# Fixed distances modulo 256 bytes between tokens, high weights and low weights in a one-core decoder layer

## The chip, the core and the metric

One core of a Trainium2 chip runs the whole layer as one program. The metric is the device time of that program in microseconds, the median over runs. A second number used below is the span of one profiled execution, from its first instruction to its last.

## The reference, cut to what matters

One decoder layer on 256 prompt tokens and 8 sample tokens, all in float32, with a model width of 2048 (16 chunks of 128).

```python
def layer(x, ...):
    xn = rmsnorm(x, g_mix)
    z = xn @ w_in                                   # all inputs of both groups
    ... RG-LRU group -> y_rg, mLSTM group -> y_ml ...
    x = x + jnp.concatenate([y_rg, y_ml], axis=-1) @ w_out
    xq = (rmsnorm(x, g_xa) @ w_xa_q)                # cross attention, 4 heads, 256 memory rows
    ...
    x = x + o @ w_xa_o
    xf = rmsnorm(x, g_ffn)
    x = x + (jax.nn.silu(xf @ w_ffn_gate) * (xf @ w_ffn_up)) @ w_ffn_down
    return x
# memory keys and values: mn @ w_k, mn @ w_v;  y = rmsnorm(x, g_final)
```

Nearly all the arithmetic is in products of a token matrix (264 columns: 256 prompt and 8 sample tokens) with a weight matrix of 128 output columns per step.

## The kernel before

**Three products for one.** Each float32 operand is split into a high part in the tensor engine's reduced float32 type and a low part that is the remainder. A product is the sum of three matmuls (`mm3`, L179): high weights with high tokens, high weights with low tokens, low weights with high tokens. In each matmul the 128x128 block of weights is loaded into the array and 264 token columns are streamed through it. Below, one *chunk* is the group of three matmuls of one 128-row block of the contraction; a step has 16 chunks (12 in the last part of the feed-forward).

**Steps.** The list `steps` holds one entry for each 128 output columns of a weight matrix (1 MB, `raw`). `load_piece` fetches it on SyncE's queue into one of three buffers, three steps ahead. `split_half(i, h)` converts it one step ahead, in two halves of 1024 columns: ScalarE writes the high half `wh`, then VectorE writes the low half `wl = raw - wh`. Each half is a tile of its own, four buffers for `wh` and four for `wl`, so a half is free again as soon as the tensor engine has used its eight chunks. `proj` (L819) walks the chunks in their natural order 0 to 15. The results are taken out of PSUM (`evac`, residual adds, gates) one step later. Between the steps `pump` hands out slices of side work (RG-LRU, mLSTM, decode attention) to ScalarE and VectorE; the framework's scheduler then fixes one order of instructions per engine.

**Where the operands lie.** A token array (`Arr`, `HL`) is cut into tiles of four chunks, `[128, 4, 264]` float32. One chunk is 1056 bytes, which is 4 x 256 + 32: the place of a chunk in its tile (its number modulo four) shifts it by 32 bytes modulo 256. All these tiles come from one ring of 26 buffers of 4224 bytes (tag `B`), which is 16.5 x 256, so that neighbouring buffers differ by 128 bytes modulo 256. A weight chunk is 512 bytes, and `wh` and `wl` tiles are 4096 bytes: in the built program every weight chunk, high or low, starts at 224 modulo 256. So the *distance*, the start of the streamed tokens less the start of the weights, modulo 256, runs through all multiples of 32, by the place of the chunk and by the buffers that the high and the low token tiles happened to get. In the text a chunk is named by the two distances of its high and its low tokens, such as (192, 64).

**Memory rows.** The 256 memory tokens use the same buffers with a chunk of 1024 bytes, so that there the distance is the same for all four chunks of a tile. In the value projections (`pe_v`) the roles are exchanged: memory rows are the loaded operand and 512 weight columns are streamed.

Two more names: `evac_rgg` and `rg_out` sum squares in `acc_rg`, the residual adds in `acc_x`; `tmp` gives short-lived tiles from a ring of `NT` buffers.

Of the kernel before, what the change touches and what calls it, by code (L numbers as in the profile page):

```python
# [10 lines left out]
F32 = mybir.dt.float32  # L11
F32R = mybir.dt.float32r
I32 = mybir.dt.int32
AF = mybir.ActivationFunctionType
# [3 lines left out]
P = 128  # L18
D = 2048
KC = D // P  # L20
T = 256
NS = 8
N = T + NS
# [57 lines left out]
def layer_kernel(ctx: ExitStack, tc, xT, memT, vec, wrg, w_in, w_out, w_q, w_k, w_v, w_o,  # L81
# [3 lines left out]
    act, dve, pe = Engine(nc.scalar, price_act), Engine(nc.vector, price_dve), Engine(nc.tensor, price_pe)  # L85
    pool_e, sp = nc.gpsimd, nc.sync
# [20 lines left out]
    def ltmp(w=N):  # L107
        return tmp(w, "lt")

    class Arr:  # L110


# [2 lines left out]

        def tile(self, q):
            if q not in self.t:
                self.t[q] = B([P, min(4, self.nb), self.w], self.dt)
            return self.t[q]

        def __call__(self, c):
            return self.tile(c // 4)[:, c % 4, :]

    class HL:
        def __init__(self, nb, w=N):
# [11 lines left out]
    steps = []  # L137
    LD, LS = 3, 1

    raws, splits = {}, {}  # L140

    def load_piece(i):
        if i >= len(steps) or i in raws:
# [6 lines left out]
    def split_half(i, h, parts=1):  # L150
        if i >= len(steps):
            return
        if steps[i][2] is pe_if:
            if h == 0:
                split_gates(i)
            return
        cols = steps[i][1]
        lo, hi = h * 1024, min(cols, (h + 1) * 1024)
# [3 lines left out]
        n = (hi - lo) // parts  # L162
        with tc.high_priority():
            for o in range(0, hi - lo, n):
                st["split"] = act.activation(wh[:, o: o + n], r[:, lo + o: lo + o + n], AF.Copy)
                dve.tensor_sub(wl[:, o: o + n], r[:, lo + o: lo + o + n], wh[:, o: o + n])
        splits[i, h] = (wh, wl)

    class W:
        def __init__(self, i):  # L170
            self.i = i

        def __call__(self, c, w=P):
            per = 1024 // w
            wh, wl = splits[self.i, c // per]
# [59 lines left out]
    def bank(tag="mm"):  # L235
        return psm.tile([P, 512], F32, tag=tag, bufs=4, name=nm(tag))

    warm_act = const.tile([P, 1], F32, name="warm_act")
    act.activation(warm_act, ones[:, 0:1], AF.Square)

    def warm(n, w=None):

# [262 lines left out]

    def split_gates(i):

        r = raws[i]
        for h in range(2):
            w = sb.tile([P, 8, P], F32R, tag="wh", bufs=4, name=nm("wh"))  # L510
            x = r[:, h * 1024: h * 1024 + 1024].rearrange("p (c m) -> p c m", m=P)
            with tc.high_priority():
                act.activation(w[:, :, 0:64], x[:, :, 0:64], AF.Copy)
                dve.tensor_sub(w[:, :, 64:128], x[:, :, 0:64], w[:, :, 0:64].bitcast(F32))
            splits[i, h] = w

    def pe_if(i):
        ps = bank()
        for c in range(KC):
            w = splits[i, c // 8][:, c % 8, :]  # L520
            xh, xl = rx(c)
            pe.matmul(ps[:, :N], w, xh, start=c == 0, stop=False)
            pe.matmul(ps[:, :N], w, xl, start=False, stop=c == KC - 1)
        return ps

    def evac_if(ps):
# [79 lines left out]
    def evac_v(j):  # L606
        def f(ps):
            if j == 0:
                ml["v"] = Arr(8)
            dve.tensor_mul(ml["v"](j), ps[:, :N], rstd)  # L610
            ml["vn"] = j + 1
        return f
# [203 lines left out]
            split(*st["yml"](j), z, V("g_ml", j))  # L816
        return f

    def proj(src, rhs, evac, cols=2048, n=N, need=()):  # L819
# [26 lines left out]
    for q in range(4):  # L846
        steps.append((w_in[q], 2048, pe_first(q), evac_first if q == 3 else None, ()))
    for n in range(4, RGB):
        proj(w_in[n], rx, evac_rgx(n))
    steps.append((w_in[8], 2048, pe_if, evac_if, ()))  # L850
    for j in range(8):
        proj(w_in[9 + j], rx, evac_qk(j))
    for j in range(8):
        proj(w_in[17 + j], rx, evac_v(j))
    for n in range(RGB):
        proj(w_in[25 + n], rx, evac_rgg(n), need=("rg",))
    for j in range(8):
        proj(w_in[33 + j], rx, evac_o(j))

# [21 lines left out]
    def final(m):  # L881

        def f(ps):
            x = xres[:, m, :]
            if m == 0:
                st["y"] = Arr(KC)
            dve.tensor_add(x, x, ps[:, :N])
            if m < KC - 1:
                sumsq(acc_x, x, m == 0)
            else:  # L890
                warm(4)
                sq = tmp()
                with tc.high_priority():
                    act.activation(sq, x, AF.Square)
                fin_sums(fin["sum"], sq, False)
            act.activation(st["y"](m), x, AF.Copy, scale=V("g_final", m))
            if m == 0:
                act.activation(warm_act, acc_x[:, 0:1], AF.Sqrt)
            elif m == KC - 2:
                fin["sum"] = bank("ax")  # L900
                fin_sums(fin["sum"], acc_x, True)
            elif m == KC - 1:
                rstd_fin(fin["sum"])
        return f

    def mem_gen():
        raw = Arr(KC, T)
        for i in range(4):
            pool_e.dma_start(raw.tile(i), memT[:, i * 4: i * 4 + 4, :])
        yield STEP  # L910
        yield STEP
        acc = ltmp(T)
        for c in range(KC):
            sumsq(acc, raw(c), c == 0)
            yield 0.35
        r = ltmp(T)
        yield STEP
        yield from rstd_from(acc, r, D)
        st["mem"] = HL(KC, T)
        for c in range(KC):  # L920
            x = raw(c)
            dve.tensor_mul(x, x, r)
            split(*st["mem"](c), x, V("g_mem", c))
            yield 0.7
# [3 lines left out]

    for m in range(KC):
        proj(w_out[m], ry, residual(m, "g_xa", "xa", norm_x),  # L930
             need=("rgout",) if m == 0 else ())

# [77 lines left out]

    rq = lambda c: st["xa"](c)
    for j in range(KC):
        proj(w_q[j], rq, evac_q(j), need=("rstd_xa",) if j == 1 else ())

    rm = lambda c: st["mem"](c)
    kv = {}
# [46 lines left out]

    def attend(h):
        qh, ql = B([P, 4, T], F32R), B([P, 4, T], F32R)
        q = qn["t"].tile(h)
        act.activation(qh, q, AF.Copy)
        dve.tensor_sub(ql, q, qh.bitcast(F32))  # L1070
        yield 1.2
# [49 lines left out]

    for h in range(H):
        for j in range(4):
            proj(w_k[4 * h + j], rm, evac_k(h, j), n=T, need=("memg",))
        for k4 in range(4):
            steps.append((w_v[h, k4], 2048, pe_v(h, k4), evac_vm(h) if k4 == 3 else None, ()))

    def ro(c):
        return st["o"](c)
# [6 lines left out]
    def pe_o(m):  # L1136
        def f(i):
            ps = bank()
            w = W(i)
            if m >= 2:  # L1140
                for c in range(KC):
                    mm3(ps[:, :N], w(c), ro(c), c == 0, c == KC - 1)
                return ps
            held[m] = (ps, w)
            for c in range(12):
                mm3(ps[:, :N], w(c), ro(c), c == 0, False)
# [49 lines left out]
    for part, nf in enumerate(FPARTS):  # L1196
        for j in range(nf):
            proj(w_gu[2 * (f0 + j)], rf, evac_gate(f0 + j, part, j),
                 need=("rstd_ffn",) if part == 0 and j == 1 else ())
            proj(w_gu[2 * (f0 + j) + 1], rf, evac_up(part, j))  # L1200
        wd = (w_d0, w_d1, w_d2)[part]
        ra = lambda c, part=part: st["a", part](c)
        lastp = part == 2
        for m in range(KC):
            proj(wd[m], ra, final(m) if lastp else residual(m, None, None, None), cols=nf * P)
        f0 += nf


# [171 lines left out]
```

## Time and profile before

| what | value |
|---|---|
| runs shown (three) | 1572.96, 1575.18, 1575.92 us; median 1575.18 |
| the profiled execution's own time | 1576.51 us |
| its span | 1574.8 us |
| granted TensorE clock, mean | 0.991 |
| matmuls busy / weight loads busy | 99% / 97% of the span |
| VectorE / ScalarE / GpSimd busy | 67% / 50% / 7% |
| 264-column matmuls with projection weights | 10,496 in groups of `wh` and `wl` |

In the rows of a group the order is: line, engine, operation, output<-inputs, shapes, count, then busy microseconds, the mean of one in ns, idle time before it and what ended that. Nearly every operation stands under line 60, since the class `Engine` records them there, so groups are told apart by tile names. The mean of one matmul (285 ns) is its latency; matmuls overlap, and what counts is the distance of their starts. Rows of the timeline give the start, the duration, and a count where equal neighbours are merged: `wh ... x2` is the first two matmuls of a chunk, so its start is the start of the chunk.

### The profile page before, as it was taken

Reading aid. Unit: us, or ns where it says so; the run is one execution under the profiler, and the core shown is the slowest. Engines: PE = TensorE matmul, PEld = TensorE weight load, DVE = VectorE, ACT = ScalarE, POOL = GpSimd, SP = SyncE. Lnnn points to the kernel's source line nnn. Section 1 sums busy time; section 2 is a strip of 40 time slices with the busy share of each in tenths; the row PEclk is TensorE's granted clock in tenths of the full one; section 3 lists DMA queues with packets and bytes.
Section 4 is the critical chain, followed back from the end, with each engine's and each line's share of the span. In section 5 each row is a group of like instructions: output and inputs, shape, how many; then the busy total and the mean of one; then the engine's idle time right before and its main releaser. Section 6 shows DMA issues by size and latency. Waiting matters only on the chain.

```text
span 1574.8 us, 29829 instructions
## 1 busy us (share of the span) xinstructions
PE 1556.5 (99%) x12340; PEld 1532.6 (97%) x12340; DVE 1051.4 (67%) x2021; ACT 789.7 (50%) x1252; POOL 109.6 (7%) x174
## 2 busy tenths in 40 slices
PE   9999999999999999999999999999999999999997
PEld 8999999999999889999999999999999999999997
DVE  7876877787699899956655555455555554555554
ACT  7465675565455656645444444333444433344463
POOL 0001210000124333200000000000000000000000
PEclk9999999999999999999999999999999999999998
DMA  8455875546689788745545555555455554555452
GB/s 304 161 174 172 294 269 205 178 145 245 248 321 346 302 305 319 251 161 178 187 164 185 188 180 175 181 188 186 174 179 186 187 181 172 184 188 184 156 179 99
DMA packets 55303, 325.97 MB, mean 207 GB/s; under 512 B 6688, under 2 KB 7120, under 8 KB 24448
## 3 DMA queue, kind: packets, MB, share of 16 engines
q1 hardware_dynamic: 39744, 270.68, 48.4%
q0 software_dynamic: 15136, 53.16, 9.4%
q8 instruction: 96, 1.57, 0.4%
q14 instruction: 39, 0.32, 0.1%
q10 hardware_dynamic: 288, 0.23, 0.1%
HBM read 312.78 MB, written 11.28 MB: 206 GB/s over the span
## 4 chain that ended last, share of the span: by engine, by line
PE 94%; DMA 2%; DVE 2%; ACT 1%; issue 1%; DVEq 0%; POOL 0%; SPq 0%; ACTq 0%
PE mm L60 89%; PE ax L60 4%; DVE B L60 1%; DMA o_sc<-B 1%; ACT B L60 1%; DMA raw<-w_in 1%; ACT wh L60 0%; DMA B<-scr 0%; DVE wl L60 0%; ACT L60 0%; DMA vecs<-vec 0%; DMA scr<-lt 0%; DVE t L60 0%; DVE dw L60 0%; ACT t L60 0%
## 5 line engine op out<-in xcount | busy, mean ns | idle before, releaser
L60 PE MATMUL mm<-B,wh 128*128 128x264 f32 (+1 forms) x7520 | 1379.0, 285 | 4.8 <-DVE B L60 3.0
L60 PEld LDWEIGHTS mm<-B,wh 128*128 128x128 f32 x7520 | 1168.4, 189 | 6.4 <-ACT cso L60 3.1
L60 PE MATMUL mm<-B,wl 128*128 128x264 f32 (+1 forms) x3744 | 1062.8, 284 | 0.6 <-DVE wl L60 0.6
L60 ACT ACTIVATE wh<-raw 128x1024 fp32r<-128x1024 f32 (+2 forms) x518 | 536.9, 1038 | 692.0 <-PE mm L60 574.6
L60 DVE TENSOR_TENSOR wl<-raw,wh 128x1024 fp32r<-128x1024 f32 (+2 forms) x516 | 619.0, 1201 | 356.7 <-ACT wh L60 350.0
L60 PEld LDWEIGHTS mm<-B,wl 128*128 128x128 f32 x3744 | 706.7, 189 | 1.1 <-DVE wl L60 1.0
L60 DVE TENSOR_TENSOR t<-mm,rstd 128x264 f32<-128x264 f32 x104 | 44.9, 432 | 60.2 <-PE mm L60 60.2
L60 PE MATMUL mm<-wh,B 128*128 128x512 f32 x256 | 82.3, 395 | 0.0
L60 DVE TENSOR_TENSOR xres<-xres,mm 128x264 f32<-128x264 f32 x80 | 34.2, 428 | 47.1 <-PE mm L60 47.1
L1272 POOL TENSOR_TENSOR B<-B,rstd 128x264 f32<-128x264 f32 x4 | 2.8, 743 | 864.9 <-ACT rstd L60 864.9
L60 PEld LDWEIGHTS mm<-wh,B 128*128 128x128 f32 x256 | 47.8, 189 | 9.8
L60 DVE SCALAR_TENSOR_TENSOR B<-B,dw 128x256 f32<-128x256 f32 x128 | 52.6, 465 | 2.3 <-ACT dw L60 2.3
L60 PE MATMUL mm<-wl,B 128*128 128x512 f32 x128 | 50.6, 395 | 0.0
L60 DVE SCALAR_TENSOR_TENSOR dw<-B,qsm,dw 128x256 f32<-128x256 f32 x96 | 47.9, 500 | 1.4 <-ACT dw L60 0.7
L60 PE MATMUL ax<-B,B 128*128 128x256 f32 (+3 forms) x288 | 48.2, 308 | 0.3 <-DVE B L60 0.3
L60 PEld LDWEIGHTS ax<-B,B 128*128 128x128 f32 x288 | 40.8, 189 | 4.0 <-issue 1.2
L977 POOL TENSOR_TENSOR ds<-dw,ds 128x256 fp32r<-128x256 f32 x32 | 35.4, 1107 | 115.3 <-ACT ds L60 115.2
L60 ACT ACTIVATE B<-xres,vecs 128x264 fp32r<-128x264 f32 (+1 forms) x64 | 31.1, 503 | 2.5 <-DMA xres<-xT 1.4
L60 ACT ACTIVATE t<-xres 128x264 f32<-128x264 f32 x60 | 23.9, 413 | 15.4 <-DVE xres L60 15.4
L60 PEld LDWEIGHTS mm<-wl,B 128*128 128x128 f32 x128 | 24.1, 188 | 5.0
L966 POOL DMA_DIRECT2D B<-kcT x32 | 17.5, 546 | 147.4 <-DVE B L60 127.0
L60 DVE TENSOR_TENSOR acc_x<-acc_x,t 128x264 f32<-128x264 f32 x59 | 25.2, 428 | 0.9 <-ACT t L60 0.5
(157 smaller groups left out, 740.0 us busy)
## 6 DMA issues: line engine op xcount, KB each, us to landing
raw<-w_gu SPq DMA_DIRECT2D x88, 1024.0 KB, 4.8
raw<-w_in SPq DMA_DIRECT2D x40, 1024.0 KB, 4.9
raw<-w_d SPq DMA_DIRECT2D x32, 1024.0 KB, 4.8
raw<-w_out SPq DMA_DIRECT2D x16, 1024.0 KB, 4.8
B<-kcT POOLq DMA_DIRECT2D x32, 512.0 KB, 6.1
raw<-w_q SPq DMA_DIRECT2D x16, 1024.0 KB, 5.0
B<-vcT POOLq DMA_DIRECT2D x32, 512.0 KB, 7.2
raw<-w_k SPq DMA_DIRECT2D x16, 1024.0 KB, 6.4
```

What stands on the lines that cost most here:

```text
L60: return f(*a, **k)
L966: pool_e.dma_start(kc, kcT[h, b])
L977: pool_e.tensor_sub(ws[:, 1], acc, ws[:, 0].bitcast(F32))
L1272: e.tensor_mul(st["y"](c), st["y"](c), r)
```

## The change

Token tiles are put into buffers of 4352 bytes (17 x 256), 64 bytes from the start. A step's whole weights are one `wh` and one `wl` tile of 8448 bytes (33 x 256), two buffers each, with the low weights 128 bytes from the start; in a tile the chunks stand in four groups by their number modulo four, each group 2080 bytes (8 x 256 + 32) after the last. The order of the chunks in a step goes group by group, forward in one step and backward in the next. In the built program all `B`, `wh` and `wl` buffers start at 160 modulo 256, so each chunk has a distance of 64 between tokens and high weights and of 192 (that is, minus 64) between tokens and low weights, whatever its place. Value projections keep natural columns (`wide`). To make room `NT` goes from 6 to 5 and `acc_rg` becomes another name of `acc_x`.

```diff
+    BW, XO = 1088, 16
+    WW, LO = 2112, 32
...
-                self.t[q] = B([P, min(4, self.nb), self.w], self.dt)
+                t = B([P, BW], self.dt)
+                self.t[q] = t[:, XO: XO + 4 * N].rearrange("p (c n) -> p c n", n=N)
...
-    NB, NT, NL, NFL = 26, 6, 3, 2
+    NB, NT, NL, NFL = 26, 5, 3, 2
...
-        wh = sb.tile([P, 1024], F32R, tag="wh", bufs=4, name=nm("wh"))
-        wl = sb.tile([P, 1024], F32R, tag="wl", bufs=4, name=nm("wl"))
+        if h == 0:
+            splits[i] = wtiles()
+        wh, wl = splits[i]
...
+        h4, l4 = wgroups(wh), wgroups(wl)
+        x = r.rearrange("p (q j m) -> p q j m", j=4, m=P)
+        q0, q1 = h * 2, min(cols // (4 * P), h * 2 + 2)
+        n = (q1 - q0) // parts or 1
         with tc.high_priority():
-            for o in range(0, hi - lo, n):
-                st["split"] = act.activation(wh[:, o: o + n], r[:, lo + o: lo + o + n], AF.Copy)
-                dve.tensor_sub(wl[:, o: o + n], r[:, lo + o: lo + o + n], wh[:, o: o + n])
-        splits[i, h] = (wh, wl)
+            for q in range(q0, q1, n):
+                k = slice(q, min(q + n, q1))
+                st["split"] = act.activation(h4[:, k], x[:, k], AF.Copy)
+                dve.tensor_sub(l4[:, k], x[:, k], h4[:, k].bitcast(F32))
+
+    def wtiles():
+        wh = sb.tile([P, WW], F32R, tag="wh", bufs=2, name=nm("wh"))
+        wl = sb.tile([P, WW], F32R, tag="wl", bufs=2, name=nm("wl"))
+        return wh[:, 0: 4 * GW], wl[:, LO: LO + 4 * GW]
+
+    GW = 4 * P + 8
+
+    def wgroups(t):
+        return t.rearrange("p (j g) -> p j g", g=GW)[:, :, 0: 4 * P].rearrange("p j (q m) -> p q j m", m=P)
+
+    def order(n, back=False):
+        return [c for j in (range(3, -1, -1) if back else range(4)) for c in range(j, n, 4)]
...
-            o = (c % per) * w
+            o = c * w if w != P else c % 4 * GW + c // 4 * P
...
-    acc_rg = const.tile([P, N], F32, name="acc_rg")
+    acc_rg = acc_x
...
-            for c in range(nch):
-                mm3(ps[:, :n], w(c), rhs(c), c == 0, c == nch - 1)
+            for k, c in enumerate(order(nch, back)):
+                mm3(ps[:, :n], w(c), rhs(c), k == 0, k == nch - 1)
```

The tensor engine, a gate or up step of the feed-forward, its first four chunks. `B` tiles hold four chunks of tokens each (1208, 1231 and so on are the high parts of the four quarters before, 995, 1012, 1034 and 1056 after; the next number is the low part). Before:

```order
L60 MATMUL mm_1347_9862<-B_1208_8715,wh_1337_9795 128x264
L60 MATMUL mm_1347_9862<-B_1209_8716,wh_1337_9795 128x264
L60 MATMUL mm_1347_9862<-B_1208_8715,wl_1338_9796 128x264
L60 MATMUL mm_1347_9862<-B_1208_8715,wh_1337_9795 128x264
L60 MATMUL mm_1347_9862<-B_1209_8716,wh_1337_9795 128x264
L60 MATMUL mm_1347_9862<-B_1208_8715,wl_1338_9796 128x264
```

After:

```order
L60 MATMUL mm_1098_9607<-B_995_8496,wh_1092_9544 128x264
L60 MATMUL mm_1098_9607<-B_996_8497,wh_1092_9544 128x264
L60 MATMUL mm_1098_9607<-B_995_8496,wl_1093_9545 128x264
L60 MATMUL mm_1098_9607<-B_1012_8691,wh_1092_9544 128x264
L60 MATMUL mm_1098_9607<-B_1013_8692,wh_1092_9544 128x264
L60 MATMUL mm_1098_9607<-B_1012_8691,wl_1093_9545 128x264
L60 MATMUL mm_1098_9607<-B_1034_8945,wh_1092_9544 128x264
L60 MATMUL mm_1098_9607<-B_1035_8946,wh_1092_9544 128x264
L60 MATMUL mm_1098_9607<-B_1034_8945,wl_1093_9545 128x264
L60 MATMUL mm_1098_9607<-B_1056_9199,wh_1092_9544 128x264
```

The number and kind of the matmuls are the same. Before, the second chunk of a step is the neighbour in the same token tile; now it is the chunk of the same place in the next tile, and the third chunk already needs the second half of the weights.

ScalarE in the output projection of the cross attention, two steps each, with what an instruction waits for. `wh ...` are the two halves of a step's conversion, `B` and `t` the tokens for the next norm's products and their squares; `PE_49`, `DVE_49` and `Activation_49` are the engines' own counters, `DMAHW...` a landed load. Before:

```order
L60 ACTIVATE wh_1285_9380<-raw_1276_9307 128x1024 [waits DMAHW2_49,PE_49,Activation_49]
L60 ACTIVATE wh_1287_9384<-raw_1276_9307 128x1024 [waits PE_49,Activation_49]
L60 ACTIVATE B_1261_9178<-xres_91,vecs_88 128x264 [waits DVE_49]
L60 ACTIVATE t_1284_9377<-xres_91 128x264
L60 ACTIVATE wh_1294_9447<-raw_1283_9372 128x1024 [waits DMAHW3_49,PE_49,Activation_49]
L60 ACTIVATE wh_1296_9451<-raw_1283_9372 128x1024 [waits PE_49,Activation_49]
```

After:

```order
L60 ACTIVATE wh_1015_8698<-raw_1006_8625 128x2x4x128 [waits DMAHW3_49,PE_49]
L60 ACTIVATE B_1012_8691<-xres_91,vecs_88 128x264 [waits DVE_49]
L60 ACTIVATE t_1014_8695<-xres_91 128x264 [waits DMASW7_49]
L60 ACTIVATE wh_1015_8698<-raw_1006_8625 128x2x4x128 [waits DVE_49]
L60 ACTIVATE wh_1020_8761<-raw_1011_8688 128x2x4x128 [waits DMAHW4_49,PE_49]
L60 ACTIVATE B_1012_8691<-xres_91,vecs_88 128x264 [waits DVE_49]
L60 ACTIVATE t_1019_8758<-xres_91 128x264 [waits DMASW0_49]
L60 ACTIVATE wh_1020_8761<-raw_1011_8688 128x2x4x128 [waits DVE_49]
```

Before, each half waits for the tensor engine by itself. Now the first half waits for the tensor engine's last use of the whole tile, and the second half, in the same tile, waits for VectorE: its counter value is the subtraction of the first half (`wl` reads the first half of `wh`).

More of the change, by code (lines that the diff above doesn't have):

```diff
@@ L138, in layer_kernel @@
     LD, LS = 3, 1
-    raws, splits = {}, {}
+    raws, splits, wide = {}, {}, set()
     def load_piece(i):
@@ L236, in bank, with warm_act @@
         return psm.tile([P, 512], F32, tag=tag, bufs=4, name=nm(tag))
-    warm_act = const.tile([P, 1], F32, name="warm_act")
-    act.activation(warm_act, ones[:, 0:1], AF.Square)
+    def warm_act(x, func):
+        t = sb.tile([P, 16], F32, tag="c", bufs=8, name=nm("c"))
+        act.activation(t[:, 0:1], x, func)
+    warm_act(ones[:, 0:1], AF.Square)
     def warm(n, w=None):
@@ L506, in split_gates @@
     def split_gates(i):
-        r = raws[i]
+        splits[i] = wtiles()
+        w4 = wgroups(splits[i][0])
+        x = raws[i].rearrange("p (q j m) -> p q j m", j=4, m=P)
         for h in range(2):
-            w = sb.tile([P, 8, P], F32R, tag="wh", bufs=4, name=nm("wh"))
-            x = r[:, h * 1024: h * 1024 + 1024].rearrange("p (c m) -> p c m", m=P)
+            k = slice(2 * h, 2 * h + 2)
             with tc.high_priority():
-                act.activation(w[:, :, 0:64], x[:, :, 0:64], AF.Copy)
-                dve.tensor_sub(w[:, :, 64:128], x[:, :, 0:64], w[:, :, 0:64].bitcast(F32))
-            splits[i, h] = w
+                act.activation(w4[:, k, :, 0:64], x[:, k, :, 0:64], AF.Copy)
+                dve.tensor_sub(w4[:, k, :, 64:128], x[:, k, :, 0:64], w4[:, k, :, 0:64].bitcast(F32))
     def pe_if(i):
         ps = bank()
-        for c in range(KC):
-            w = splits[i, c // 8][:, c % 8, :]
+        for k, c in enumerate(order(KC)):
+            w = W(i)(c)[0]
             xh, xl = rx(c)
-            pe.matmul(ps[:, :N], w, xh, start=c == 0, stop=False)
-            pe.matmul(ps[:, :N], w, xl, start=False, stop=c == KC - 1)
+            pe.matmul(ps[:, :N], w, xh, start=k == 0, stop=False)
+            pe.matmul(ps[:, :N], w, xl, start=False, stop=k == KC - 1)
         return ps
@@ L908, in mem_gen @@
         for i in range(4):
-            pool_e.dma_start(raw.tile(i), memT[:, i * 4: i * 4 + 4, :])
+            pool_e.dma_start(raw.tile(i)[:, :, :T], memT[:, i * 4: i * 4 + 4, :])
         yield STEP
@@ L1067, in attend @@
         qh, ql = B([P, 4, T], F32R), B([P, 4, T], F32R)
-        q = qn["t"].tile(h)
+        q = qn["t"].tile(h)[:, :, :T]
         act.activation(qh, q, AF.Copy)
@@ L1140, in f @@
             if m >= 2:
-                for c in range(KC):
-                    mm3(ps[:, :N], w(c), ro(c), c == 0, c == KC - 1)
+                for k, c in enumerate(order(KC, m % 2 == 1)):
+                    mm3(ps[:, :N], w(c), ro(c), k == 0, k == KC - 1)
                 return ps
             held[m] = (ps, w)
-            for c in range(12):
-                mm3(ps[:, :N], w(c), ro(c), c == 0, False)
+            for k, c in enumerate(order(12)):
+                mm3(ps[:, :N], w(c), ro(c), k == 0, False)
             if m == 0:
```

39 lines of the change are left out of this document (22 added, 17 removed).

## The prediction

> **What bounds the kernel now.** I read the page's engine shares first, then the groups by shape, then busy time by stage, and last the tensor engine's timeline chunk by chunk.
>
> ```profile
> span 1574.8 us, 29829 instructions
> PE 1556.5 (99%) x12340; PEld 1532.6 (97%) x12340; DVE 1051.4 (67%) x2021; ACT 789.7 (50%) x1252; POOL 109.6 (7%) x174
> L60 PE MATMUL mm<-B,wh 128*128 128x264 f32 x7008 | 1286.0, 285 | 4.1 <-DVE B L60 3.0 <-ACT wh L60 1.1
> L60 PE MATMUL mm<-B,wl 128*128 128x264 f32 x3488 | 991.1, 284 | 0.6 <-DVE wl L60 0.6
> L60 PE MATMUL mm<-B,wh 128*128 128x256 f32 x512 | 93.1, 281 | 0.6 <-ACT B L60 0.5
> 0.00:50.00 50.00, 43.96 (x322) 42.86 (x323) 38.60 (x103) 32.70 (x72) 0.95 (x7) 0.97 0.79 293
> 126.00:190.00 64.00, 63.04 (x465) 59.79 (x465) 48.72 (x136) 37.12 (x79) 12.39 (x23) 0.95 0.78 249
> 500.00:560.00 60.00, 59.87 (x414) 55.52 (x414) 53.35 (x134) 36.00 (x68) 18.35 (x27) 1.00 0.85 328
> 560.00:620.00 60.00, 59.48 (x393) 54.21 (x392) 57.57 (x158) 38.57 (x83) 19.87 (x29) 1.00 0.83 303
> 760.00:900.00 140.00, 140.00 (x1159) 140.00 (x1158) 81.88 (x115) 63.05 (x80) 0.00 (x0) 1.00 0.52 181
> 900.00:1100.00 200.00, 200.00 (x1653) 200.00 (x1653) 106.09 (x122) 79.31 (x87) 0.00 (x0) 1.00 0.51 180
> ```
>
> The tensor engine is busy all the time, and the idle time before its two large groups is 4.1 and 0.6 us. In the window rows (engines in the order PE, PEld, DVE, ACT, POOL, then granted clock, DMA share, GB/s) it is never free after the start: 1,653 matmuls in 200.00 us are one every 121.0 ns, at a clock of 1.00. No wait can be removed there; only that interval can. The groups hold 7,008 + 3,488 = 10,496 of these matmuls, so one nanosecond less is 10.5 us. Is 121.0 ns fixed by 264 columns? The timeline says no. Below stand chunks 10 and 13 of the first and of the last of 88 feed-forward steps with the same operand addresses, each as a pair of rows, the start of the chunk and of the next one (chunks counted from the step's first matmul); behind them chunks 14 and 15 of one step of the input projection, and chunk 14 of one step of the first down projection:
>
> ```profile
> 796.01 0.40 PE L60 MATMUL mm<-B,wh 128*128 128x264 f32 x2
> 796.37 0.41 PE L60 MATMUL mm<-B,wh 128*128 128x264 f32 x2
> 797.10 0.41 PE L60 MATMUL mm<-B,wh 128*128 128x264 f32 x2
> 797.48 0.40 PE L60 MATMUL mm<-B,wh 128*128 128x264 f32 x2
> ...
> 1488.79 0.40 PE L60 MATMUL mm<-B,wh 128*128 128x264 f32 x2
> 1489.14 0.41 PE L60 MATMUL mm<-B,wh 128*128 128x264 f32 x2
> 1489.88 0.41 PE L60 MATMUL mm<-B,wh 128*128 128x264 f32 x2
> 1490.25 0.40 PE L60 MATMUL mm<-B,wh 128*128 128x264 f32 x2
> ...
> 297.01 0.40 PE L60 MATMUL mm<-B,wh 128*128 128x264 f32 x2
> 297.36 0.41 PE L60 MATMUL mm<-B,wh 128*128 128x264 f32 x2
> 297.73 0.28 PE L60 MATMUL mm<-B,wh 128*128 128x264 f32 x1
> ...
> 1007.92 0.41 PE L60 MATMUL mm<-B,wh 128*128 128x264 f32 x2
> 1008.28 0.41 PE L60 MATMUL mm<-B,wh 128*128 128x264 f32 x2
> ```
>
> In these 88 steps chunk 10 takes 0.36 and 0.35 us, chunk 13 0.38 and 0.37: over all 88, from starts in whole nanoseconds, 354.1 and 371.7 ns, hardly one nanosecond of spread. Same instructions, same shapes, no waits, one PSUM bank; what differs is where the operands lie. Chunk 10 has the distances (192, 64), chunk 13 (160, 160). In the input projection chunk 14, at (64, 192), takes 0.35 us and chunk 15, at (96, 224), 0.37. Of the sixteen pairs of distances that occur, the means over the run go from 355.6 ns at (64, 192) and 357.2 at (192, 64) to 370.0 at (96, 224) and (160, 160); the mean over all is 363.5, or 121.2 per matmul. A matmul's start follows best from the distances between the tokens now streamed and the weights loaded for the next matmul, taken over three matmuls in a row (they explain 54% of the variance; one distance alone 8%).
>
> **The change part by part.**
>
> *Distances.* At (64, 192) the tokens stand, against the weights that are loaded meanwhile, at 64, 192, 64. The change makes precisely this sequence everywhere: high tokens while `wh` is loaded again 64, low tokens while `wl` is loaded 192, high tokens while the next `wh` is loaded 64. So I price every chunk by those at (64, 192) now. The majority of them takes 351 to 352 ns, chunk 14 above 353.3 as a mean of 24 steps, chunk 10 at (192, 64) 354.1. I take 353 (117.7 per matmul): 121.0 - 117.7 = 3.3 ns, times 10,496 = 34.6 us less. Bounds: the pair is also seen at 0.36 us, in the step at 1007.92 (361 ns in all 16 steps of that stage, where the chunks before it differ), 120.3 per matmul and 7 us; and in a run of equal chunks it may be quicker than among strangers. For that there is a row pair, the memory keys, where the distances stay at (0, 128) for eight chunks on end:
>
> ```profile
> 664.27 0.40 PE L60 MATMUL mm<-B,wh 128*128 128x256 f32 x2
> 667.07 0.40 PE L60 MATMUL mm<-B,wh 128*128 128x256 f32 x2
> ```
>
> 2.80 / 8 = 350 ns, by columns 264/256 x 350 = 361, while (0, 128) among other distances takes 366.3: 5 ns less. 353 less 5 to 7 is 346 to 348, 115.3 at best, 60 us. That same row also says that a fixed distance is no gain by itself; it has to be the right one.
>
> *Order by groups.* It keeps the sequence from breaking. Three times a step the group changes, and one distance is off by 32: some 200 x 3 matmuls at about 5 ns (of the 6 between 117.7 and the 123.9 of chunk 13), 3 us more. The turn of direction costs nothing. The newest token chunk of a step that follows a norm or a gate (15, or 11) is still the last used, since those steps go forward.
>
> *Memory keys and values.* 768 matmuls of 256 columns leave a pair of 117 ns; at best 2 us less, at worst as much more; I take 0. The 384 wide ones get eight changing distances; 0, within 1.
>
> *One tile per step.* This is the cost. In the feed-forward before:
>
> ```profile
> 901.29 1.06 ACT L60 ACTIVATE wh<-raw 128x1024 fp32r<-128x1024 f32 x1 [1.46 <-PE mm L60]
> 904.21 1.06 ACT L60 ACTIVATE wh<-raw 128x1024 fp32r<-128x1024 f32 x1 [1.86 <-PE mm L60]
> 902.38 1.23 DVE L60 TENSOR_TENSOR wl<-raw,wh 128x1024 fp32r<-128x1024 f32 x1 [1.31 <-ACT wh L60]
> ACT wh L60 <- PE mm L60: 574.6, 365, 4.1
> ```
>
> The halves start half a step apart, 2.92 us, each as its buffer is freed, and low weights are ready 6.5 us ahead of use. Now both are freed at the end of a step and run as a chain, since the second half on ScalarE waits for VectorE's first: 1.06 + 1.23 + 1.06 + 1.23 = 4.6 us, some 4.9 with hand-overs, within a step of 48 x 117.7 = 5.65 us; the second half is wanted two chunks later still, 0.7. So about 1.4 us are left where VectorE has little else (81.88 of 140 us busy): nothing is lost in the feed-forward, half of the run. It is lost where VectorE is full. From 500 to 620 us it is busy 53.35 and 57.57 of 60. In its new order only some steps have side work between the two subtractions; in the others it stands idle while ScalarE converts the second half, on average 0.4 us a step over the 32 steps of the memory keys and values, 12 us of idle time; the two rows leave 9 and their neighbours more. I put 3 us on the tensor engine (0 to 10). At the start (PE 43.96 of 50) loads, token conversion and weights are equally tight and the first split piece is 512 instead of 256 columns: 1.5 us (0 to 4).
>
> *Small things.* One temporary less, one sum of squares under another's name (its users lie hundreds of microseconds apart), conversions with strided output: same element counts, 0, hidden under the tensor engine; if a strided conversion were 10% slower, the chain takes 0.5 us of the 1.4.
>
> Sum: -34.6 + 3 + 3 + 1.5 = -27. The profiled execution took 1576.5 for a span of 1574.8, 1.3 above the median of 1575.2; 1576.5 - 27.1 = 1549.4, on the scale of the median **1548 us**.
>
> **The rivals.**
>
> *Addresses do not matter.* The Trainium skill, "SBUF — State Buffer", section "Who interferes with whom", says that PE and ACT never wait on anyone and gives the tensor engine independent read ports for weights and for streamed operands. By that rule no distance could change a matmul and the sum would be only the costs, 4.5 us slower. As a mechanism here: the 354 and 372 ns would belong to something that the change does not move with the distance, such as the token buffers' own addresses (all weights start at 224 now, so the rows cannot tell distance from address). Then all goes on at about 363 ns: 1575.2 + 4.5 = 1580. The rows speak against the rule as far as they go, since no such spread should exist; they leave the address open. Chance 0.09.
>
> *The whole tile stalls the tensor engine.* The chain takes 4.9 of 5.65 us and has 1.4 us to spare; where side work stands between its links and adds 2 us, the next step starts 0.6 us late. In the about 75 steps with side work (to 250 us, and from 414 to 680) that is 45 us against 32 without such losses: 1575.2 - 32 + 45 = 1588. It decides from 0.43 us a step. For it: VectorE's 57.57 of 60. Against it: the feed-forward's 81.88 of 140. Chance 0.08.
>
> *The sequence locks at the slow step.* (64, 192) also occurs at 361 ns; if all chunks settle there, the gain is 7 and with the costs the time is 1575.2 - 7 + 5 = 1573, or 1565 if half do. Chance 0.10. If they settled at the slow end, 370, it would be 2.3 x 10,496 = 24 us more: 1604. Chance 0.04.
>
> **How the numbers follow.** My forecast has 0.69. Its own ends: 60 us less and costs of about 5, 1520; 119.3 per matmul (358 ns, 18 us) and costs of 13, 1570. The range of 1520 to 1581 holds it, the slow lock and most of the first rival. What a measurement of this kernel can tell is about 0.2%, 3.2 us. Faster by more: forecast, slow lock: 0.79. Within: a third of the first rival, 0.03. Slower: 0.18.
>
> **What would show it.** Right: some 1,700 matmuls in 200 us of the feed-forward instead of 1,653; all chunks of a step equal to a nanosecond or two; ScalarE's second conversion waiting for VectorE; small gaps before `wh` and `wl` matmuls from 500 to 620 us and before 40 us. Wrong: 1,653 again (the address rival), or an idle time before the `wh` and `wl` groups of tens of microseconds (the stall).

## The result and the profile after

| kernel | median, us | runs | ratio to before, 95% interval |
|---|---|---|---|
| before | 1575.55 | 4 (1572.96 to 1576.59) | 1 |
| changed | 1584.01 | 4 (1582.99 to 1584.32) | 1.0055 [1.0038, 1.0072] |

Slower by half a per cent; the forecast was 1548, and its range ended at 1581. The page of the changed kernel, the two groups by shape, the same windows as before, and the waits (engine and tile that waits, what it waits for, total us, times, longest):

```profile
span 1582.3 us, 29581 instructions
PE 1555.0 (98%) x12340; PEld 1528.0 (97%) x12340; DVE 1053.3 (67%) x2019; ACT 785.0 (50%) x1248; POOL 106.2 (7%) x174
...
L60 PE MATMUL mm<-B,wh 128*128 128x264 f32 x7008 | 1282.2, 285 | 8.1 <-ACT wh L60 5.0 <-ACT cso L60 3.0
L60 PE MATMUL mm<-B,wl 128*128 128x264 f32 x3488 | 995.2, 286 | 6.2 <-DVE wl L60 6.2
...
0.00:50.00 50.00, 44.08 (x326) 43.50 (x327) 37.76 (x99) 32.46 (x70) 0.94 (x7) 1.00 0.76 280
50.00:126.00 76.00, 72.78 (x528) 69.71 (x527) 65.39 (x148) 46.33 (x84) 2.34 (x4) 0.93 0.38 131
300.00:360.00 60.00, 54.39 (x430) 53.39 (x429) 49.40 (x102) 35.27 (x66) 0.55 (x1) 0.94 0.47 165
500.00:560.00 60.00, 60.00 (x419) 55.70 (x418) 55.76 (x143) 37.40 (x74) 20.82 (x32) 1.00 0.90 341
560.00:620.00 60.00, 60.00 (x418) 55.59 (x418) 54.20 (x144) 37.77 (x77) 16.89 (x28) 1.00 0.84 308
680.00:760.00 80.00, 77.76 (x562) 73.03 (x561) 45.42 (x71) 38.25 (x62) 1.08 (x2) 1.00 0.46 165
900.00:1100.00 200.00, 200.00 (x1662) 200.00 (x1661) 106.66 (x122) 79.71 (x87) 0.00 (x0) 1.00 0.51 180
...
ACT wh L60 <- PE mm L60: 472.2, 214, 7.8
DVE wl L60 <- ACT wh L60: 241.3, 315, 3.2
ACT wh L60 <- DVE wl L60: 187.3, 200, 2.2
```

Of before, the three windows that the prediction did not show:

```profile
50.00:126.00 76.00, 75.08 (x575) 73.63 (x573) 60.04 (x136) 48.07 (x82) 2.33 (x4) 0.97 0.40 139
300.00:360.00 60.00, 60.00 (x497) 60.00 (x496) 50.24 (x105) 38.81 (x71) 0.53 (x1) 1.00 0.46 160
680.00:760.00 80.00, 80.00 (x611) 77.58 (x610) 48.28 (x73) 39.51 (x63) 1.08 (x2) 1.00 0.48 165
```

Two things stand here. In the feed-forward 1,662 matmuls run in 200 us instead of 1,653: 120.3 ns for 121.0, not 117.7. And the tensor engine, full in both later windows before, now idles 5.6 us between 300 and 360 (granted clock 0.94) and 2.2 between 680 and 760, and 3.2 instead of 0.9 between 50 and 126 (clock 0.93 instead of 0.97). Where the forecast had put its small gaps, 500 to 620 us, it is busy all 120.

Of the signs that the forecast named, ScalarE's second conversion does wait for VectorE (the last row above), but the chunks of a step are not equal. Starts of chunks in one forward step of the feed-forward, the first three and the sixth and seventh:

```profile
908.06 0.40 PE L60 MATMUL mm<-B,wh 128*128 128x264 f32 x2
908.43 0.40 PE L60 MATMUL mm<-B,wh 128*128 128x264 f32 x2
908.78 0.41 PE L60 MATMUL mm<-B,wh 128*128 128x264 f32 x2
...
909.86 0.42 PE L60 MATMUL mm<-B,wh 128*128 128x264 f32 x2
910.24 0.40 PE L60 MATMUL mm<-B,wh 128*128 128x264 f32 x2
```

By the starts in whole nanoseconds, the first chunk of 63 such steps takes 363.3 ns, the second 356.7, the sixth 374.1, all at the same two distances. The first two make 720.0 together, which is twice 360.0: what one chunk gains the next one pays. The sixth's extra 14 ns no neighbour makes good.

Summed over the starts of all 10,496 matmuls (an interval over 160 ns counts as 121 ns and a stall, intervals in half-clock stretches apart): the mean interval goes from 121.17 to 120.63 ns, 5.7 us less; stalls go from 5.0 to 19.0 us, 14.0 more; the half clock (stretches in which the profile grants half of the tensor engine's clock) costs 9.3 instead of 7.7, 1.7 more before rounding; all other matmuls take 2.7 less. Together 7.3 more, for 7.5 in the spans. While the changed kernel's matmuls run, the half clock sets in at 49.9, 118.2 and 350.3 us, each time during idle time of the tensor engine or within 1.5 us behind it (3.0, 2.0 and 4.0 us), and at 241.1 us, 1.1 us behind 24 matmuls of one column.

The largest stall, in the timeline of the changed kernel:

```profile
338.31 5.11 DVE L60 TENSOR_TENSOR B<-B,lt 128x256 f32<-128x256 f32 x15
...
345.20 1.22 DVE L60 TENSOR_TENSOR wl<-raw,wh 128x1024 fp32r<-128x1024 f32 x1
...
346.33 3.65 DVE L60 SCALAR_TENSOR_TENSOR B<-B,vecs,B 128x256 fp32r<-128x256 f32 x9
...
346.46 1.04 ACT L60 ACTIVATE wh<-raw 128x1024 fp32r<-128x1024 f32 x1
...
347.56 0.51 PE L60 MATMUL mm<-B,wh 128*128 128x264 f32 x2 [0.33 <-ACT wh L60]
...
352.17 1.23 DVE L60 TENSOR_TENSOR wl<-raw,wh 128x1024 fp32r<-128x1024 f32 x1
...
353.43 1.06 ACT L60 ACTIVATE wh<-raw 128x1024 fp32r<-128x1024 f32 x1 [2.24 <-DVE wl L60]
353.45 0.28 PEld L60 LDWEIGHTS mm<-B,wl 128*128 128x128 f32 x1 [4.25 <-DVE wl L60]
353.45 0.59 PE L60 MATMUL mm<-B,wl 128*128 128x264 f32 x1 [4.04 <-DVE wl L60]
```

VectorE works through the normalisation of the memory rows, 15 products and then the splits of the sixteen chunks, in the order fixed beforehand. The step that the tensor engine begins at 345.67 has its first half of the weights alone, and its third chunk already needs the second, which ScalarE converts at 347.81. By the names in the built program, the scheduler has put the first chunk of the next step there. The half that ScalarE converts for it at 346.46 (the tensor engine takes up its high weights at 347.56) gets its subtraction only at 352.17, behind that work; the tensor engine has waited 4.04 us for the low weights when it goes on at 353.45, and ScalarE's conversion of the other half starts only then. Before, the halves came free half a step apart and each served eight chunks, and the same work fitted between (60.00 of 60 us busy).

### The profile page after: what moved, and what is told of

Read it like the earlier page. It is cut to its first block, busy times and chain, and to the rows that moved or that the text cites. A ratio compares the mean times of both kernels' runs of the same rounds, so it can differ in the third digit from the quotient of the medians.

```text
span 1582.3 us, 29581 instructions
## 1 busy us (share of the span) xinstructions
PE 1555.0 (98%) x12340; PEld 1528.0 (97%) x12340; DVE 1053.3 (67%) x2019; ACT 785.0 (50%) x1248; POOL 106.2 (7%) x174
## 4 chain that ended last, share of the span: by engine, by line
PE 96%; DVE 2%; ACT 1%; DMA 0%; issue 0%; DVEq 0%; SPq 0%
PE mm L60 90%; PE ax L60 5%; DVE B L60 1%; DVE wl L60 1%; ACT wh L60 1%; ACT B L60 1%; DMA raw<-w_in 0%; ACT L60 0%; DVE c L60 0%; DVE xres L60 0%; ACT t L60 0%; DVE acc_x L60 0%; DVE t L60 0%; DVEq L1394 0%; ACT rstd L60 0%
## 5 line engine op out<-in xcount | busy, mean ns | idle before, releaser
L60 ACT ACTIVATE wh<-raw 128x1024 fp32r<-128x1024 f32 (+1 forms) x516 | 534.1, 1042 | 696.3 <-PE mm L60 472.2
L60 DVE TENSOR_TENSOR wl<-raw,wh 128x1024 fp32r<-128x1024 f32 (+1 forms) x514 | 616.0, 1204 | 245.9 <-ACT wh L60 241.3
L1012 POOL TENSOR_TENSOR ds<-dw,ds 128x256 fp32r<-128x256 f32 x32 | 31.0, 968 | 111.9 <-ACT ds L60 111.8
```

The costliest lines, as they stand in the source:

```text
L60: return f(*a, **k)
L1012: pool_e.tensor_sub(ws[:, 1], acc, ws[:, 0].bitcast(F32))
```

## The experiments

Theory: the tensor engine keeps to a pace of its own in any even sequence, near 120 ns, so that the right distance has little to give (*lock*), and the loss is the whole tile (*whole tile*). Rivals: (64, 192) is fast and something spoils it; the loss comes from the order by groups, from the common release of both halves, or from the buffers given up for space. In the code cuts `...` stands for what is left out, and what follows `#` is a note of this text.

**Matmuls alone (e1_bench).** The layer is left out; each segment is one list of places, weights `w` and tokens `x` in one large tile, streamed 264 columns at a time unless said otherwise:

```diff
+        for k, (w, x) in enumerate(seq):
+            pe.matmul(ps[:, :n], R[:, w: w + P], R[:, x: x + n], start=k == 0, stop=k == len(seq) - 1)
```

> Leaves the layer out: only matmuls back to back over zeros in one tile, in segments, each with fixed places of weights and tokens; nothing runs on the other engines meanwhile. The interval of matmuls of 264 columns is read for each segment (first dozen left out). Theory lock: a steady repetition of one distance settles near 120 ns, whatever pair it is, and the 353 ns chunks of the old kernel were fast only because the chunks ahead of them were slow; so the triple at (64, 192) takes 359 to 361 ns per chunk, and no pair of the 64 is below 357. Rival disturbed: (64, 192) is a fast pair by itself, 352 to 354 ns, and in the changed kernel the group changes or the slots' places modulo 512 spoil it; then the segments with the changed kernel's own places take 360 to 362 and one of those with other slot sizes 353 to 355. Rival address: the interval changes when both places move together at a fixed distance, by up to 5 ns.

Timeline rows, each one segment: one fixed distance of 0, then of 32; the triple at fixed (64, 192); two steps with the changed kernel's own moving places; at last one fixed distance with 128, 264 and 384 columns:

```profile
17.89 4.57 PE L144 MATMUL mm<-R 128*128 128x264 f32 x36
...
22.33 4.64 PE L144 MATMUL mm<-R 128*128 128x264 f32 x36
...
263.76 4.62 PE L144 MATMUL mm<-R 128*128 128x264 f32 x36
...
452.78 11.83 PE L144 MATMUL mm<-R 128*128 128x264 f32 x96
...
546.52 4.21 PE L144 MATMUL mm<-R 128*128 128x128 f32 x36
...
563.57 4.57 PE L144 MATMUL mm<-R 128*128 128x264 f32 x36
...
572.44 6.51 PE L144 MATMUL mm<-R 128*128 128x384 f32 x36
```

From the starts, without the first dozen of each segment: distance 0 gives 120.0 ns, every interval alike; 32 gives 122.25; the row repeats after 256 bytes. Of the 64 pairs (high, low) the triple takes 359.9 to 373.2 ns, mean 364.8. (64, 192) takes 364.8 when it is all there is, with high and low weights at one place modulo 256 as in the kernel before: an average pair. The changed kernel's own places (low weights 128 bytes off) give 120.56, where the layer has 120.63 over the run, although VectorE and ScalarE, but for the zeroing at the start, stand idle: the other engines do not set this pace. With 264 columns no segment goes below 119.8. So the floor holds, and 353 is the steady chunk of no pair here; nor do other slot sizes bring it back, at 120.6 per matmul (the *disturbed* rival). The *address* rival's 5 ns do not show either: with both places moved together at a distance of 64, seven of eight places give 121.0 and one 120.0. A part of the theory fell too, which had any one distance near 120 and (64, 192) at 359 to 361.

**Two tiles of two groups (e2_half).** Distances, order and token slots of the changed kernel, halves apart again. A half is now two whole groups, so that the first eight chunks of a step need one half alone, where in the changed kernel the third chunk needs the second half:

```diff
-        wh = sb.tile([P, WW], F32R, tag="wh", bufs=2, name=nm("wh"))
-        wl = sb.tile([P, WW], F32R, tag="wl", bufs=2, name=nm("wl"))
-        return wh[:, 0: 4 * GW], wl[:, LO: LO + 4 * GW]
+        w = sb.tile([P, WW], F32R, tag="wh", bufs=4, name=nm("wh"))   # high and low of half a step
+        o = 16 * h
+        return w[:, o: o + 2 * GW], w[:, LO + o: LO + o + 2 * GW]     # LO = 1056
```

> The changed kernel, but a step's weights in two tiles of two groups each, four buffers, so that each half is freed and converted by itself as in the kernel before; distances, order and token slots as in the changed kernel. Theory whole tile: the idle time before the wh and wl groups (8.1 and 6.2 us) and the throttled clock behind it come from the chain of four conversions; they go back to about 4 and 1 us, and the time is 1584 less 12 to 15, so 1569 to 1572, with 1,662 matmuls in 200 us as now. Rival order: the groups' order makes a step want its late token chunks early; then the gaps stay and the time is 1580 to 1585.

1567.72, 1 us below what the theory gave, ratio to before 0.9953 [0.9941, 0.9966]; `wl` counts as `wh` in its views, since both lie in one tile:

```profile
300.00:360.00 60.00, 59.05 (x490) 58.84 (x489) 51.90 (x106) 39.67 (x73) 0.55 (x1) 1.00 0.44 160
900.00:1100.00 200.00, 200.00 (x1661) 200.00 (x1660) 106.64 (x122) 78.84 (x87) 0.00 (x0) 1.00 0.51 182
```

The interval is the changed kernel's (120.63 over the run); stalls fall from 19.0 to 8.9 us and the half clock's cost from 9.3 to 4.1. The order by groups is still there, so it is not what stalled for the most part; 8.9 is still 3.9 above before, with 3.6 less of half clock.

**Only the padded slots (e3_pads).** The kernel before with the change's token slots, low weights at a fixed place behind the high ones, five temporaries and the shared sum of squares:

```diff
-                self.t[q] = B([P, min(4, self.nb), self.w], self.dt)
+                t = B([P, BW], self.dt)
+                self.t[q] = t[:, XO: XO + 4 * N].rearrange("p (c n) -> p c n", n=N)
...
+        w = sb.tile([P, WW], F32R, tag="wh", bufs=4, name=nm("wh"))
+        wh, wl = w[:, 0: 1024], w[:, LO: LO + 1024]
```

> The kernel before, with only the padded slots and low weights at a fixed place against the high ones; natural order, two half tiles as before, one temporary less and the shared sum of squares as in the change. Distances go round through four pairs, (64,192), (96,224), (128,0), (160,32), instead of staying. Theory lock: any steady sequence is near 120 to 121 ns; no stalls; 1568 to 1576. Rival pairs: each chunk takes what its pair took in the kernel before, (64,192) 355.6 but (96,224) 370.0, mean near 364; 1576 to 1582. Rival space: the temporary less and the shared buffer cause the gaps at 115 and 345 us; 1580 to 1585 with those gaps.

1574.68, ratio 0.9999 [0.9990, 1.0007], stalls 5.1 us as before: what was given up for space costs nothing that shows.

```profile
900.00:1100.00 200.00, 200.00 (x1653) 200.00 (x1653) 106.20 (x121) 78.79 (x87) 0.00 (x0) 1.00 0.51 182
```

From the starts, the four chunks of a round take 360.8, 367.5, 362.5 and 362.5 ns in the feed-forward. The pair (64, 192), 355.6 on average among the sixteen of before, is 360.8 here and 364.8 alone: it has no price of its own.

**Only the whole tile (e4_whole).** The kernel before, its two natural halves in one tile:

```diff
-        wh = sb.tile([P, 1024], F32R, tag="wh", bufs=4, name=nm("wh"))
+        if h == 0:
+            both[i] = (sb.tile([P, 2048], F32R, tag="wh", bufs=2, name=nm("wh")), ...)
+        wh, wl = (t[:, h * 1024: h * 1024 + 1024] for t in both[i])
```

> The kernel before, with a step's two halves in one tile of high and one of low weights, two buffers each; places, order and distances hardly moved (low weights as before at a multiple of 256 bytes). The halves are stretches that do not overlap, so ScalarE's second conversion needs not wait for VectorE's first. Theory whole tile: freeing both halves only at the step's end costs as in the changed kernel, 1575.5 + 10 to 14 = 1586 to 1590, with gaps near 115, 345 and 717 us. Rival overlap: it is the wait of the second conversion for the first subtraction, which the groups' interleaved places bring, that makes the chain too long; without it 1576 to 1580. Rival order: nothing, 1574 to 1577.

1578.71, ratio 1.0028 [1.0019, 1.0038]. Neither 1586 nor nothing: it is the *overlap* rival that fits. (`issue` is time in which an engine waits for nothing that the profile shows.)

```profile
300.00:360.00 60.00, 58.39 (x476) 57.76 (x476) 53.35 (x110) 39.11 (x72) 0.53 (x1) 1.00 0.52 185
560.00:620.00 60.00, 55.57 (x362) 51.06 (x361) 52.24 (x144) 35.08 (x78) 18.30 (x27) 0.97 0.75 278
...
ACT wh L60 <- issue: 424.4, 129, 4.5
```

The wait of `wh` for `wl` has gone from the list; stalls are 11.5 us, and the half clock costs 1.4. Its gaps include one that the changed kernel does not have, 4.4 us from 560 to 620.

**Whole tiles without the chain (e6_nochain).** The changed kernel; each conversion now fills two whole groups rather than half of all four, so the places of the two no longer interleave:

```diff
+            J = slice(2 * h, 2 * h + 2)
+                st["split"] = act.activation(h4[:, :nq, J], x[:, :nq, J], AF.Copy)
+                dve.tensor_sub(l4[:, :nq, J], x[:, :nq, J], h4[:, :nq, J].bitcast(F32))
...
+        for h in (1, 0) if i + LS in rev else (0, 1):      # rev: backward steps
+            split_half(i + LS, h)
```

> The changed kernel with its whole tiles, but each conversion takes two groups of the tile in place of half the weights spread over all four groups, so that the two conversions' places don't overlap and ScalarE's second needs not wait for VectorE's first; backward steps convert their groups in the order of use. Both halves still come free together at the step's end. Theory interleaving: most of the loss is that wait; the time is 1568 to 1574. Rival freeing: the loss is the common release at the step's end; 1578 to 1584 with the gaps at 115 and 345 us left. The two-tile kernel took 1567.7, so what lies between is the price of the common release.

1569.50, ratio 0.9966 [0.9952, 0.9979], 14.5 us less than the changed kernel:

```profile
300.00:360.00 60.00, 58.31 (x480) 57.68 (x479) 52.86 (x109) 39.30 (x72) 0.55 (x1) 1.00 0.52 185
900.00:1100.00 200.00, 200.00 (x1661) 200.00 (x1660) 104.55 (x123) 76.27 (x89) 0.00 (x0) 1.00 0.51 183
...
ACT wh L60 <- issue: 414.9, 128, 4.3
ACT wh L60 <- PE mm L60: 231.1, 94, 4.6
```

187.3 us of waits of ScalarE for VectorE are gone, stalls are 9.4 us and the half clock's cost 4.3. ScalarE now converts both halves one after the other, and the subtractions follow when VectorE comes to them. New gaps of 2.7 us stand between 500 and 620 us. Between this and e2_half lie 1.8 us, with places and order nearly the same; their intervals overlap, so the price of the common release is small and not clear of noise. What cost 16 us was for the most part the interleaved layout. It brings two things, ScalarE's wait for VectorE and a third chunk that needs the second half; both are gone here, and no run parts them.

**Moving places, 64 pairs (e5_bench_moving).**

> Leaves the layer out: matmuls alone, as in e1_bench, but each segment is two steps of 16 chunks whose places move as in the changed kernel, for all 64 pairs of distances, held in groups of four (64 segments), held over all 16 chunks by padding each weight chunk by 32 bytes (64 segments), and eight pairs in groups with the second step backward. Theory lock: no pair goes below 120.0 ns per matmul; (128,128) is near 120.1 in groups; held over all 16 chunks a good pair is 120.0; (64,192) in groups forward is about 120.6 and the spread over pairs is that of fixed places, 120 to 124.4. Rival movement: once the places move, all pairs come to 120.5 to 121.5 and the choice is worth nothing.

With places that move as in the kernel (forward, in groups) the pairs go from 120.1 to 122.7 ns, mean 121.8; for the first four segments the records don't tell the ends apart. (128, 128) takes 120.10, (64, 192) 120.83, which is 362.5 per chunk at the very places modulo 256 where the kernel before had 355.6 among other pairs. With the distance held over all 16 chunks the best are 119.96 and 120.02, the worst 123.24, the mean 121.8, and (128, 128) takes 120.70. So the choice is worth up to 2.6 ns in groups and 3.3 held, the floor stays, and neither theory's figure for the spread, 120 to 124.4 or 120.5 to 121.5, is right.

**A bad and a good pair in the layer (e7_slow_pair, e8_fwd128).** e2_half with token offsets `XH, XL` in the slots of high and low tokens:

```diff
     BW, XO = 1088, 16
+    XH, XL = 32, 32        # e7: distances (128, 0)
+    XH, XL = 32, 0         # e8: distances (128, 128), all steps forward
```

> The two-tile kernel (1567.7) with the tokens 64 bytes further on in their slots, so that the distances are (128, 0) in place of (64, 192): the slowest pair of the measurement at fixed places, 373.2 ns per chunk. Theory distances matter by the table: (373.2 - 361.7) / 3 = 3.8 ns on 10,496 matmuls, 40 us more: 1600 to 1610. Rival: with moving places the pair says little; 1565 to 1575.

> The two-tile kernel (1567.7) with high tokens 64 bytes further on and low tokens 64 bytes less, so that all three distances of a chunk are 128, and with all steps forward. At fixed and at moving places the matmuls alone took 120.0 ns there, with one or two ns at a change of group. Theory lock: 120.1 to 120.2 per matmul against 120.56, 4 to 5 us less: 1562 to 1564, with 1,664 to 1,667 matmuls in 200 us of feed-forward. Rival: as before within 1 us.

e7 took 1578.50, ratio 1.0022 [1.0013, 1.0031]; e8 1588.86, ratio 1.0083 [1.0069, 1.0096]. Both expectations missed. Their feed-forwards, e7 and then e8:

```profile
900.00:1100.00 200.00, 200.00 (x1647) 200.00 (x1646) 105.76 (x122) 78.33 (x87) 0.00 (x0) 1.00 0.53 183
```

```profile
900.00:1100.00 200.00, 200.00 (x1633) 200.00 (x1633) 104.95 (x120) 77.66 (x87) 0.00 (x0) 1.00 0.49 179
```

Over the run a matmul takes 121.63 and 122.63 ns, 1.0 and 2.0 more than in e2_half; times 10,496 that is 10.5 and 21.0, and the medians moved by 10.8 and 21.1 (the profiled executions, from which the starts are, by 7.5 and 20.0, with fewer stalls in e7). Nothing but addresses was changed in e7. So addresses do set the time, but the two distances don't name the state: in the measurement alone, (128, 128) had high and low weights at one place modulo 256 and high and low tokens at one place; in e8 they lie 128 bytes apart.

**The good pair at the right places (e9_phase).**

```diff
-    XH, XL = 32, 0
-    WW, LO = 2112, 1056
-    GW = 4 * P + 8
+    XH, XL = 32, 32
+    WW, LO = 2112, 512     # each low group 512 elements, 8 x 256 bytes, behind its high group
+    GW = 8 * P + 8
```

> As e8, distances 128 throughout and all steps forward, but with high and low weights in one place modulo 256 bytes (each low group stands 512 bytes behind its high group) and high and low tokens in one place too, as the matmuls alone had it when they took 120.1 ns at (128,128); in e8 high and low lay 128 bytes apart, and a matmul took 122.65. Theory history: a matmul depends on more than the distance to the next weights, on the places of the loads before it too; with the places of the measurement alone its 120.1 to 120.2 comes back: 1567.7 - 0.4 x 10,496 = 1563, and 1,664 matmuls or more in 200 us of feed-forward. Rival: the layer around it, not the places, made e8's 122.65; then 1585 to 1590 again.

(The 512 of that text are elements: 2048 bytes.) 1562.34 us, ratio 0.9924 [0.9910, 0.9937], the fastest of all:

```profile
900.00:1100.00 200.00, 200.00 (x1667) 200.00 (x1666) 107.72 (x125) 79.30 (x89) 0.00 (x0) 1.00 0.52 183
```

From the starts, chunks of the feed-forward are 360.0 to 360.3 ns except at the change of group; over the run a matmul takes 120.30. Against e2_half that is 3.4 us of pace, and stalls and half clock take 2.7 less. As expected, with the layer around it the matmuls nearly keep the pace that they have alone at these places (120.10). From e8 to e9 nothing but places was changed, and that is 26.5 us.

## Why the prediction was wrong

**Distances, the step that failed.** The term was -34.6 us; the interval gave 5.7, and the 900 to 1100 us window 0.66 ns x 10,496 = 6.9. The reading of the spread as addresses was right (e1, e7 to e9), and so was the sequence 64, 192, 64 in the program. Wrong was to price a steady sequence by a chunk of a mixed one. Chunk 10's 354 ns stood among slower ones, and a start-to-start time belongs partly to the neighbours, as the 363.3 and 356.7 ns of the changed kernel's first two chunks show, which make 720.0. That a matmul which starts early or late against the loads passes this on to the next would explain it; no run shows how. In a steady sequence the pair is 364.8 at fixed places, 362.5 at moving ones and 361.7 as the change lays it; at the best places a chunk is 360.0. The row of the memory keys, 350 ns by columns 361, was the only steady sequence in the trace and said 120.3; it was used to push the lower end down, where it should have been the value. That it fits so well is partly luck: matmuls alone do not scale by columns in this way (at the distance 0, 256 and 264 columns take the same 120.0 ns; at 64, 117.7 and 121.0). What came is the third rival's lock at 361, with its gain of 7; its time, 1573, was missed for the cost that follows.

**One tile per step, the second failure.** 3 us were forecast, with ends 0 and 10; against e2_half the changed kernel loses 16.3. The chain was seen rightly, and the early need of the second half was put into the sum (0.7 us): ScalarE waits for VectorE 200 times, 187.3 us in all, and the feed-forward loses nothing (200.00 of 200). Where it hurts was misjudged: by the average busy share of VectorE, which pointed to 500 to 620 us. It hurts most where a stretch of side work stands in VectorE's fixed order between two links, at 338 to 357 us; at 300 to 360 VectorE was busy only 50.24 of 60 before. At 717 to 723 us the whole tiles of two steps come free together: ScalarE has waited 3.02 us for the tensor engine when it converts both first halves at 717.54. At 112 to 130 us the tensor engine idles 3.2 us, but 3.4 in e6_nochain as well, so there the layout is at most a part of the cause. And a stall has a second price that no term held: the half clock, 5 us of the difference to e2_half (against before, 1.7). The second rival had the mechanism, but as a little in each of 75 steps, where it was a few stalls. That its 1588 is near 1584 is luck: it took a gain of 32 us, where 5.7 came, and a loss of 45, where stalls and half clock took 15.7 more.

**Right or small.** At the start the changed kernel is busy 44.08 of 50 us against 43.96: 1.5 were forecast, none shows. The order by groups is inside the measured pace; e2_half, which has it, takes 13.0 us for stalls and half clock, and before took 12.7. Memory keys and values at 0: the other matmuls together took 2.7 less. The shared sum and the temporary less: nothing, by e3_pads.

**The first rival** fell. The Trainium skill, "SBUF — State Buffer", section "Who interferes with whom", says that PE never waits on anyone, and its table gives weight loads a read port independent of the streamed operand's. That no other engine slows the matmuls, the runs bear out at the changed kernel's places (120.56 ns alone, 120.63 in the layer). But with the other engines idle, the same matmuls take 120.0 to 124.4 ns by how tokens and weights lie to each other (moved together, they keep 121.0 in seven of eight places), for which independent ports leave no room. What in the memory does that, no run shows. That this rival's 1580 is nearer than 1548 is luck too: it had no gain in pace and only 4.5 us of costs.

What stays open: which address relations set the pace. Three offsets (high tokens, low tokens and low weights, against the high weights) and the movement can matter; the measurements alone covered the first two fully, with low weights at one place with the high ones. Open is also which of the two things that the interleaved layout brings, the wait or the early need of the second half, costs how much.

## What to carry to other kernels

A duration taken between strangers is not the price of the same thing in a row of its own: look in the trace for a stretch that is already steady, or measure one, before multiplying by ten thousand. Interleaving two halves in one buffer can make a new dependency, and can make the second half wanted sooner; the price is not the mean slack of a step but the longest run of other work in the waiting engine's order, and the clock after it. Two changes in one can hide each other: here the pace was worth 6 to 7 us and the layout cost 16. Parting them gave a kernel that is 0.5% faster than before, and the places that the matmuls alone had shown to be best made it 0.8%.

## What the runs showed of the hardware

Back to back, alone and at a good place, a matmul with 264 columns takes 120.0 ns, exactly even; 256 columns take the same, 128 columns take 111.7, 384 take 173.3 and 512 take 226.7 at the distance 0. From 384 to 512 a column costs 0.417 ns, by which 128 columns would take 67: there something other than the stream sets the pace. The Trainium skill, "TensorE: Matmul & The Clock Gate", section "LDWEIGHTS (loading the stationary operand)", gives P / 1.2 ns for P columns of weights, by estimate 107 for 128. The 111.7 here is near that, as it would be if the weight load set the pace, though no run takes the load away to show it. A bad pair costs up to 4% of a matmul's time (124.4 against 120.0 ns alone) and shows nowhere as a wait, since the tensor engine counts as busy throughout.
